# Up projection of a gated MLP: seven block products for eight over 6 of its 16 contraction tiles, with weight sums and two gating steps on POOL

## The chip, the cores and the metric

One core of a Trainium2 chip runs the whole layer in one launch. The metric is the device time of one execution in microseconds (us). The engines are PE (matmuls; PEld is its weight load), DVE, ACT, POOL and SP, which here only issues DMAs.

## What is computed

One layer of a diffusion block over 512 latent tokens, width 2048, in fp32. The part that matters here is the gated MLP at the end:

```
z = h @ w_up
grid = z.reshape(bsz, rows, GRID_W, 2 * D_FF)
...
val, gate = jnp.split(grid.reshape(bsz, n, 2 * D_FF), 2, axis=-1)
return (val * jax.nn.silu(gate)) @ w_down
```

`h` is 512 x 2048, `D_FF` is 5632, and the line left out is a depthwise 3 x 3 convolution over the 8 x 64 grid of tokens. The block's output is normalized and scaled by a row that comes from a product of the conditioning vector with a part of `w_ada`.

## The kernel before, in words

Every fp32 product is made of three matmuls (`mm3`, L175 to L178): both operands are split into a high and a low part, and hi x hi, hi x lo and lo x hi are added up in one PSUM bank. The split of activations is kept; weights are split on the way. `Stream` holds a list of weight **pages** in the order of use. `load` issues the DMA of a page into one of two `raw` tiles, `make` writes its high part on ACT (`whi`, L77) and the rest on DVE (`wlo`, L78). There are two `whi` and two `wlo` tiles, so the split of a page can begin only when PE has finished the page two before it, and `get` emits it one page ahead. All DMAs of pages are issued by SP, in order.

The hidden width is cut into 44 **blocks** of 128 channels. A block i has a value half (j = 0) and a gate half (j = 1). `up(i)` computes both: 4 pages of 1024 columns, 16 contraction tiles x 3 matmuls of 512 columns for each half, then ACT copies the bank into a padded tile `zp` (L1345). `conv(i)` does the 9 taps of both halves on DVE (L1309, L1311: 18 instructions), the SiLU on ACT (L1316), the product of the halves on DVE (L1318) and the split of the result `g` on ACT and DVE (L1323, L1325). `down(gi, d)` multiplies a group of four blocks with a quarter of `w_down`: 2 pages, 48 matmuls, four banks, which `evict` adds to `facc` on DVE (L1359). `up` and `down` alternate from block 5 on (`sched`); blocks 2 to 4, 42 and 43 have no `down` beside them, and five `down`s follow block 43.

Side work on DVE and ACT is written as generators and handed to `Threads`. `tick(us)` after some matmuls lets them emit as much work as 0.65 of that time pays for; `finish` emits a thread to its end at once. So the order on each engine is fixed when the program is built. One such thread is `gemv5`: 64 dot products on DVE (L975) of loaded rows of `w_ada` (`gv` tiles of 256 KB) with a row `srow2`, then `rows_of`, which turns the result into the rows `frow` that the last evictions need: DVE makes diagonals `dg`, PE multiplies them with ones (`rowb`), ACT copies them out. It is added before block 2 with the lowest priority.

Blocks 0 and 1 are computed earlier, in halves of 256 tokens (`up_half`, tiles `uh`).

## Time and profile before

| | |
|---|---|
| runs before | 2173.89, 2174.99, 2179.12 us (median 2174.99) |
| the profiled execution | 2177.72 us, its span 2175.9 us |
| busy share of the span | PE 97%, PEld 76%, DVE 69%, ACT 32%, POOL 11% |
| mean granted clock of PE | 0.983 of full |
| DMA | 315 MB, mean 145 GB/s |

The span is the time from the first to the last instruction. A busy PE is not a PE at its peak, since matmuls are pipelined: the distance between the starts of two matmuls says more than the duration of one. The MLP begins near 720 us and holds two thirds of the span.

### The profile page before, as it was taken

The numbers are of one execution on the slowest core, as the hardware profiler recorded it, in microseconds if no ns is written. First come the engines' busy times: TensorE is split into PE (matmuls) and PEld (weight loads), VectorE is DVE, ScalarE is ACT, GpSimd is POOL, SyncE is SP. The second block draws the span as 40 slices with busy tenths as digits, with TensorE's granted clock in tenths as the row PEclk, the third lists the DMA queues.
The fourth block names the chain that finished last, engine by engine and source line by source line (L and its number), as shares of the span: only waits on it lengthen the run. The fifth ranks groups of instructions, "written<-read, shape, count | busy, mean of one in ns | idle before, by whom it ended". The sixth has DMA issues, their size and how long they took to land.

```text
span 2175.9 us, 25243 instructions
## 1 busy us (share of the span) xinstructions
PE 2102.5 (97%) x9708; PEld 1645.7 (76%) x9708; DVE 1493.3 (69%) x2183; ACT 694.4 (32%) x976; POOL 243.8 (11%) x311
## 2 busy tenths in 40 slices
PE   7998999999898999999999999999999999999996
PEld 3575777767777888888888888888888888888885
DVE  1573488436677788778778777676776767767676
ACT  3343424544356323322222222222222222222224
POOL 5951100142025000000000000000000000000004
PEclk8999999999999999999999999999999999999998
DMA  9876454657665223443343333232332233232225
GB/s 371 311 285 218 136 178 145 205 150 206 223 211 204 78 88 127 144 140 119 109 154 124 124 126 112 88 97 88 97 97 92 93 97 93 92 97 97 92 93 193
DMA packets 107672, 315.05 MB, mean 145 GB/s; under 512 B 15520, under 2 KB 21536, under 8 KB 103328
## 3 DMA queue, kind: packets, MB, share of 16 engines
q1 hardware_dynamic: 99776, 303.39, 42.0%
q10 hardware_dynamic: 7776, 10.06, 1.4%
q8 instruction: 76, 1.25, 0.2%
q14 instruction: 44, 0.36, 0.0%
HBM read 302.46 MB, written 10.94 MB: 144 GB/s over the span
## 4 chain that ended last, share of the span: by engine, by line
PE 65%; DVE 2%; ACT 1%; issue 1%; DMA 1%; DVEq 0%; POOL 0%; ACTq 0%
PE up L176 14%; PE up L178 14%; PE up L177 14%; PE dn L177 7%; PE dn L178 7%; PE dn L176 7%; ACT scr L1124 1%; DMA raw<-in_w_up 0%; PE uh L178 0%; DMA raw<-in_w_down 0%; DVE facc L1126 0%; PE uh L177 0%; PE uh L176 0%; DVE wlo L78 0%; DVE hf L1195 0%
## 5 line engine op out<-in xcount | busy, mean ns | idle before, releaser
L78 DVE TENSOR_TENSOR wlo<-raw,whi 128x1024 fp32r<-128x1024 f32 (+1 forms) x326 | 403.6, 1239 | 456.7 <-ACT whi L77 453.9
L77 ACT ACTIVATE whi<-raw 128x1024 fp32r<-128x1024 f32 (+1 forms) x326 | 341.5, 1048 | 787.2 <-PE dn L178 308.6
L1311 DVE SCALAR_TENSOR_TENSOR cv<-zp,wconv,cv 128x512 f32<-128x512 f32 x704 | 528.4, 751 | 18.8
L176 PE MATMUL up<-h,whi 128*128 128x512 f32 x1344 | 531.4, 395 | 0.0
L178 PE MATMUL up<-h,wlo 128*128 128x512 f32 x1344 | 530.9, 395 | 0.0
L177 PE MATMUL up<-h,whi 128*128 128x512 f32 x1344 | 530.8, 395 | 0.0
L178 PEld LDWEIGHTS up<-h,wlo 128*128 128x128 f32 x1344 | 251.9, 187 | 61.8
L176 PEld LDWEIGHTS up<-h,whi 128*128 128x128 f32 x1344 | 252.0, 187 | 61.4
L177 PEld LDWEIGHTS up<-h,whi 128*128 128x128 f32 x1344 | 251.9, 187 | 61.4
L177 PE MATMUL dn<-wlo,g 128*128 128x512 f32 x672 | 265.5, 395 | 0.0
L178 PE MATMUL dn<-whi,g 128*128 128x512 f32 x672 | 265.4, 395 | 0.0
L176 PE MATMUL dn<-whi,g 128*128 128x512 f32 x672 | 265.4, 395 | 0.0
L1126 POOL TENSOR_TENSOR facc<-facc,frow 128x512 f32<-128x512 f32 x11 | 15.4, 1422 | 1435.1 <-ACT scr L1124 1435.1
L1345 ACT ACTIVATE zp<-up 128x512 f32<-128x512 f32 x84 | 50.5, 601 | 378.5 <-PE up L178 378.5
L177 PEld LDWEIGHTS dn<-wlo,g 128*128 128x128 f32 x672 | 126.0, 187 | 30.8
L176 PEld LDWEIGHTS dn<-whi,g 128*128 128x128 f32 x672 | 125.9, 187 | 30.9
L178 PEld LDWEIGHTS dn<-whi,g 128*128 128x128 f32 x672 | 126.0, 187 | 30.7
L975 DVE SCALAR_TENSOR_TENSOR scr<-gv,srow 128x512 bf16<-128x512 f32 x132 | 97.4, 738 | 17.8 <-DMA gv<-in_ada_n 11.1
L1359 DVE TENSOR_TENSOR facc<-facc,dn 128x512 f32<-128x512 f32 x144 | 92.1, 680 | 0.7 <-PE dn L178 0.7
L176 PE MATMUL ub<-hT,whi 128*128 128x512 f32 x192 | 79.4, 414 | 1.9 <-ACT mt L585 1.9
L176 PE MATMUL wo<-whi,mx 128*128 128x512 f32 x192 | 79.5, 414 | 0.0
L177 PE MATMUL wo<-wlo,mx 128*128 128x512 f32 x192 | 77.4, 403 | 0.9 <-DVE wlo L78 0.9
(285 smaller groups left out, 2434.4 us busy)
## 6 DMA issues: line engine op xcount, KB each, us to landing
raw<-in_w_up SPq DMA_DIRECT2D x176, 512.0 KB
raw<-in_w_down SPq DMA_DIRECT2D x88, 512.0 KB
gv<-in_ada_n SPq DMA_DIRECT2D x132, 256.0 KB
adak<-in_ada_k SPq DMA_DIRECT2D x32, 1024.0 KB
gv<-in_ada_m SPq DMA_DIRECT2D x96, 256.0 KB
raw<-in_w_out SPq DMA_DIRECT2D x32, 512.0 KB
raw<-in_w_inp SPq DMA_DIRECT2D x24, 512.0 KB
adag<-in_ada_n SPq DMA_DIRECT2D x7, 1024.0 KB
```

The costliest lines, as they stand in the source:

```text
L77: nc.scalar.activation(hi[:, :n], raw[:, :n], AF.Copy)
L78: nc.vector.tensor_tensor(lo[:, :n], raw[:, :n], hi[:, :n].bitcast(F32), op=OP.subtract)
L176: PE.matmul(o, ahi, bhi, start=start, stop=False)
L177: PE.matmul(o, ahi, blo, start=False, stop=False)
L178: PE.matmul(o, alo, bhi, start=False, stop=stop)
L975: V.scalar_tensor_tensor(scr[:, :512], tiles[x][:], 1.0, row(qf), op0=OP.mult, op1=OP.mult, accum_out=gacc[:, qf, c, nt:nt + 1])
L1124: S.activation(scr[:, :512], m, AF.Square, accum_out=st8[:, t, d:d + 1])
L1126: eng.tensor_tensor(m, m, row[d // 2][:, d % 2, :], op=OP.mult)
L1311: V.scalar_tensor_tensor(a[:], zz, wcol, a[:], op0=OP.mult, op1=OP.add)
L1345: S.activation(zp[j][i % 2][:, 1:9, 1:65], o.rearrange("p (r c) -> p r c", r=8), AF.Copy)
L1359: V.tensor_tensor(f, f, os[t], op=OP.add)
```

## The change

From block 4 on (`NS`), `up7(i)` takes the place of `up(i)`. Of the 16 contraction tiles, six (three of each half, `SW` = 3, brought to the front by `ORD`) are multiplied as 2 x 2 block matrices in Winograd's form of Strassen's scheme: rows are the value and gate half, columns are tokens 0 to 255 (`H0`) and 256 to 511 (`H1`), and the two contraction halves are the three tiles of each. Seven products of 3 tiles x 3 matmuls with 256 columns replace eight. The other ten tiles stay plain, in four pages of 640 columns. Sums of the activations are made once on POOL (`hsums`, in two parts before block 4), sums of the weights for each block on POOL (`make`, four instructions behind page `sb`), and the sums of the products by `csums` on DVE, from four banks into `zp`. Two steps of `conv` go from DVE to POOL. The weights of the six tiles come as a pair of tiles of 768 columns, one pair at a time (`load_pair`). `gemv5` begins before block 4 and has two `gv` tiles where it had four; `rows_of` follows block 43.

```
+            if key[0] == "sb":
+                (a11, a12), (a21, a22) = [(t[:, :SW * 128], t[:, SW * 128:]) for t in self.pair[key[1]]]
+                nc.gpsimd.tensor_tensor(a22, a21, a22, op=OP.add)
+                nc.gpsimd.tensor_tensor(a21, a11, a21, op=OP.subtract)
+                nc.gpsimd.tensor_tensor(a11, a22, a11, op=OP.subtract)
+                nc.gpsimd.tensor_tensor(a12, a12, a11, op=OP.subtract)
+            nxt = self.pairs.get(key)
+            if nxt is not None:
+                self.load_pair(*nxt)
...
+            pages += [(("up", i, 0), up[0]), (("sa", i), None), (("up", i, 2), up[2]), (("sb", i), None)]
+            pages += [(("up", i, 1), up[1]), (("up", i, 3), up[3]), (("sA", i), None), (("sB", i), None)]
...
+    W.pairs = {("sB", i): (i + 1, [A["w_ups"][i + 1 - NS, m] for m in range(2)]) for i in range(NS, NP - 1)}
...
     def conv(i):
         for j in range(2):
+            while i > 1 - j and not cth[i - 2 + j][2]:
+                bg._step(cth[i - 2 + j])
...
-        V.tensor_tensor(res[0][:], res[0][:], res[1][:], op=OP.mult)
+        PO.tensor_tensor(res[0][:], res[0][:], res[1][:], op=OP.mult)
...
-        V.tensor_tensor(g[:, 1, :], f, g[:, 0, :].bitcast(F32), op=OP.subtract)
+        PO.tensor_tensor(g[:, 1, :], f, g[:, 0, :].bitcast(F32), op=OP.subtract)
...
+    def csums(i, bk):
+        S.activation(z0[:, ha], v(p16[:, H0]), AF.Copy)
+        V.tensor_tensor(z1[:, ha], z0[:, ha], v(p16[:, H1]), op=OP.add)
+        V.tensor_tensor(z0[:, hb], z1[:, ha], v(p57[:, H0]), op=OP.add)
+        V.tensor_tensor(z1[:, ha], z1[:, ha], v(p57[:, H1]), op=OP.add)
+        V.tensor_tensor(z1[:, hb], z1[:, ha], v(p57[:, H0]), op=OP.add)
+        V.tensor_tensor(z0, z0, v(p23), op=OP.add)
+        V.tensor_tensor(z1, z1, v(yy), op=OP.add)
+        yield from conv(i)
...
+    def up7(i):
+        plain(p23, 0, 0)
+        w = W.get(("sa", i))
+        half(p16[:, H0], w, 0, lambda p: h2o[p][:, :, H0], True, False)
+        half(p23[:, H0], w, 1, lambda p: h2o[SW + p][:, :, H0], False, False)
+        plain(yy, 1, 0)
+        w = W.get(("sb", i))
+        half(yy[:, H0], w, 1, lambda p: tt["p", p][2], False, False)
+        plain(p23, 0, 1)
+        plain(yy, 1, 1)
+        w = W.get(("sA", i))
+        half(p16[:, H1], w, 0, lambda p: tt["p", p][1], False, True)
+        half(p23[:, H1], w, 1, lambda p: h2o[SW + p][:, :, H1], False, True)
+        w = W.get(("sB", i))
+        half(p57[:, H0], w, 1, lambda p: h2o[p][:, :, H1], True, False)
+        half(p57[:, H1], w, 0, lambda p: tt["p", p][0], False, True)
+        cth[i] = bg.add(csums(i, bk), 1)
+        if i == NP - 1:
+            fr2.append(bg.add(frows(), 0))
+    def frows():
+        bg.finish(g5_t)
+        while NP - 1 not in summed:
+            bg._step(cth[NP - 1])
+        yield from rows_of(3, frow, p2, "srow2", 1)
...
+            if x[1] == NH:
+                hs_t = bg.add(hsums(False), 0)
...
+            if x[1] == NS:
+                bg.finish(bg.add(hsums(True), 0))
+                g5_t = bg.add(gemv5(), 3)
```

`half` runs 3 tiles x 3 matmuls of 256 columns, `plain` 5 tiles x 3 of 512. In the names below, `up0`, `up2`, `up1`, `up3` are the four plain pages in their new order, `sa`, `sb`, `sA`, `sB` the pages made of the pair, `dn0` and `dn1` the two pages of a `down`.

**The order inside a block, on DVE.** Before (in the names: `cv` is a convolution, `facc` the sum of the down projection):

```order
L78 TENSOR_TENSOR wlo<-raw,whi 128x1024
L1311 SCALAR_TENSOR_TENSOR cv_11018<-zp_5553,wconv,cv_11018 128x512 x5
L78 TENSOR_TENSOR wlo<-raw,whi 128x1024
L1311 SCALAR_TENSOR_TENSOR cv_11018<-zp_5553,wconv,cv_11018 128x512
L1309 TENSOR_SCALAR cv_11080<-zp_5555,wconv 128x512
L1311 SCALAR_TENSOR_TENSOR cv_11080<-zp_5555,wconv,cv_11080 128x512
L1359 TENSOR_TENSOR facc_6407<-facc_6407,dn_11022 128x512
L1359 TENSOR_TENSOR facc_6408<-facc_6408,dn_11023 128x512
L1359 TENSOR_TENSOR facc_6409<-facc_6409,dn_11024 128x512
L78 TENSOR_TENSOR wlo<-raw,whi 128x1024
L1359 TENSOR_TENSOR facc_6410<-facc_6410,dn_11025 128x512
```

In the changed kernel, the same engine from page `sa` to page `sA` (`rs` are the tiles of the pair):

```order
L98 TENSOR_TENSOR wlo<-rs_12143,whi 128x768
L1401 SCALAR_TENSOR_TENSOR cv_12255<-zp_5553,wconv,cv_12255 128x512 x3
L98 TENSOR_TENSOR wlo<-raw,whi 128x640
L1401 SCALAR_TENSOR_TENSOR cv_12255<-zp_5553,wconv,cv_12255 128x512 x2
L98 TENSOR_TENSOR wlo<-rs_12144,whi 128x384
L1399 TENSOR_SCALAR cv_12351<-zp_5555,wconv 128x512
L1401 SCALAR_TENSOR_TENSOR cv_12351<-zp_5555,wconv,cv_12351 128x512 x2
L98 TENSOR_TENSOR wlo<-raw,whi 128x640
L1401 SCALAR_TENSOR_TENSOR cv_12351<-zp_5555,wconv,cv_12351 128x512
L98 TENSOR_TENSOR wlo<-raw,whi 128x640
L1401 SCALAR_TENSOR_TENSOR cv_12351<-zp_5555,wconv,cv_12351 128x512 x3
L98 TENSOR_TENSOR wlo<-rs_12143,whi 128x768
```

POOL, which had nothing between 4 memsets at the start of the MLP and the last evictions, in the changed kernel over the same block:

```order
L1408 TENSOR_TENSOR cv_12533<-cv_12533,cv_12629 128x512
L1415 TENSOR_TENSOR g<-cv_12533,g 128x512
L103 TENSOR_TENSOR rs_12700<-rs_12700 128x384
L104 TENSOR_TENSOR rs_12700<-rs_12699,rs_12700 128x384
L105 TENSOR_TENSOR rs_12699<-rs_12700,rs_12699 128x384
L106 TENSOR_TENSOR rs_12699<-rs_12699 128x384
```

Eight splits stand where four stood in a block's `up`, and the weight sums lie on POOL between the splits of `sb` and `sA`.

**The order of the loads, on SP.** Before, where the dot products still run:

```order
L172 DMA gv<-in_ada_n 128x512 x2
L60 DMA raw<-in_w_down 128x1024
L172 DMA gv<-in_ada_n 128x512
L60 DMA raw<-in_w_up 128x1024 x4
L172 DMA gv<-in_ada_n 128x512
L60 DMA raw<-in_w_down 128x1024 x2
```

In the changed kernel, one block:

```order
L68 DMA raw<-in_w_up 128x640
L204 DMA gv<-in_ada_n 128x512
L68 DMA raw<-in_w_up 128x640 x3
L68 DMA raw<-in_w_down 128x1024
L74 DMA rs_15760<-in_w_ups 128x768
L74 DMA rs_15761<-in_w_ups 128x768
L68 DMA raw<-in_w_down 128x1024
```

The pair of the next block is loaded between the two pages of the `down`.

**The end of `gemv5`, on DVE.** Before, its last dot product is row 956 of 1481, in the middle of the MLP, and behind block 43 stand only convolution, `facc` and splits:

```order
L1311 SCALAR_TENSOR_TENSOR cv_14854<-zp_5553,wconv,cv_14854 128x512 x3
L1359 TENSOR_TENSOR facc_6407<-facc_6407,dn_14857 128x512
L1359 TENSOR_TENSOR facc_6408<-facc_6408,dn_14858 128x512
L1359 TENSOR_TENSOR facc_6409<-facc_6409,dn_14859 128x512
L78 TENSOR_TENSOR wlo<-raw,whi 128x1024
L1359 TENSOR_TENSOR facc_6410<-facc_6410,dn_14860 128x512
L1309 TENSOR_SCALAR cv_14956<-zp_5555,wconv 128x512
```

In the changed kernel there is one dot product in each block, and behind block 43, after the split of `dn1`:

```order
L98 TENSOR_TENSOR wlo<-raw,whi 128x1024
L1015 SCALAR_TENSOR_TENSOR scr,gacc<-gv,srow_14436 128x512 x7
L1015 SCALAR_TENSOR_TENSOR scr,gacc<-gv,srow_17167 128x512 x16
L1059 TENSOR_TENSOR gacc<-gacc 128x2x16
L1060 TENSOR_TENSOR acol<-gacc 128x16
L1061 TENSOR_TENSOR acol<-acol,colp 128x16
L1063 TENSOR_TENSOR acol<-acol,colp 128x16
L1437 TENSOR_TENSOR zp_5555<-zp_5553,u_16926 128x4x64
L1438 TENSOR_TENSOR zp_5553<-zp_5555,u_16928 128x4x64
L1440 TENSOR_TENSOR zp_5555<-zp_5555,u_16928 128x4x64
L1441 TENSOR_TENSOR zp_5555<-zp_5555,u_16928 128x4x64
L1443 TENSOR_TENSOR zp_5553<-zp_5553,u_16927 128x8x64
```

23 of the 64 dot products now stand together; the diagonals `dg` follow two rows further down. On PE, the first `rowb` that reads them stands behind page `dn0` of the first `down` after block 43:

```order
L208 MATMUL dn_17129<-whi,g 128x512
L209 MATMUL dn_17129<-wlo,g 128x512
L210 MATMUL dn_17129<-whi,g 128x512
L1128 MATMUL rowb<-dg,ones 128x128 x4
L208 MATMUL dn_17126<-whi,g 128x512
```

Before, all `rowb` matmuls stood in the middle of the MLP.

## Rows read from the trace of the kernel before

**Rows 1.** Page, part 1: busy time, share of the span, instructions.
```profile
PE 2102.5 (97%) x9708; PEld 1645.7 (76%) x9708; DVE 1493.3 (69%) x2183; ACT 694.4 (32%) x976; POOL 243.8 (11%) x311
```
**Rows 2.** One stretch of the MLP: us; busy PE, PEld, DVE, ACT, POOL; clock; DMA share; GB/s.
```profile
1600.00:1800.00 200.00, 200.00 (x858) 160.65 (x857) 139.67 (x180) 49.49 (x60) 0.00 (x0) 1.00 0.30 95
```
**Rows 3.** Timeline of PE, end of blocks 0 and 1 (256 columns), start of block 2.
```profile
701.54 0.28 PE L176 MATMUL uh<-h,whi 128*128 128x256 f32 x1
...
720.79 0.39 PE L176 MATMUL up<-h,whi 128*128 128x512 f32 x1
...
727.32 0.40 PE L177 MATMUL up<-h,whi 128*128 128x512 f32 x1
```
**Rows 4.** Groups of DVE by form: count | busy us, mean ns | idle before, releasers.
```profile
L1311 DVE SCALAR_TENSOR_TENSOR cv<-zp,wconv,cv 128x512 f32<-128x512 f32 x704 | 528.4, 751 | 18.8
L975 DVE SCALAR_TENSOR_TENSOR scr<-gv,srow 128x512 bf16<-128x512 f32 x132 | 97.4, 738 | 17.8 <-DMA gv<-in_ada_n 11.1 <-ACT srow L1289 4.1 <-ACT scr L1124 0.9
L1359 DVE TENSOR_TENSOR facc<-facc,dn 128x512 f32<-128x512 f32 x144 | 92.1, 680 | 0.7 <-PE dn L178 0.7
L1195 DVE TENSOR_SCALAR hf<-h2p,acol 128x256 f32<-128x256 f32 x16 | 8.6, 538 | 1.3 <-POOL h L1197 1.3
L78 DVE TENSOR_TENSOR wlo<-raw,whi 128x768 fp32r<-128x768 f32 x4 | 3.8, 955 | 1.2 <-ACT whi L77 1.2
L78 DVE TENSOR_TENSOR wlo<-raw,whi 128x384 fp32r<-128x384 f32 x4 | 2.2, 552 | 0.5 <-ACT whi L77 0.5
```
**Rows 5.** Timeline of DVE inside one block of the MLP: start us, us, instruction, [idle before].
```profile
1700.03 1.23 DVE L78 TENSOR_TENSOR wlo<-raw,whi 128x1024 fp32r<-128x1024 f32 x1 [0.73 <-ACT whi L77]
1701.17 0.68 DVE L1359 TENSOR_TENSOR facc<-facc,dn 128x512 f32<-128x512 f32 x1
1701.77 3.10 DVE L1311 SCALAR_TENSOR_TENSOR cv<-zp,wconv,cv 128x512 f32<-128x512 f32 x4
...
1729.18 0.75 DVE L1311 SCALAR_TENSOR_TENSOR cv<-zp,wconv,cv 128x512 f32<-128x512 f32 x1
1729.84 0.48 DVE L1309 TENSOR_SCALAR cv<-zp,wconv 128x512 f32<-128x512 f32 x1
```
**Rows 6.** Timeline of DVE in the first stage, with POOL at work.
```profile
118.27 1.60 DVE L476 SCALAR_TENSOR_TENSOR xl<-xl,scsh,rst 128x512 f32<-128x512 f32 x1
119.79 1.60 DVE L484 SCALAR_TENSOR_TENSOR hT<-xl,scsh,hT 128x512 fp32r<-128x512 f32 x1
121.31 1.76 DVE L476 SCALAR_TENSOR_TENSOR xl<-xl,scsh,rst 128x512 f32<-128x512 f32 x1
```
**Rows 7.** Timeline of POOL: the same stretch, and the start of the last evictions.
```profile
117.75 1.56 POOL L564 TENSOR_TENSOR mi<-bb,pio 128x512 f32<-128x512 f32 x1
119.28 1.56 POOL L564 TENSOR_TENSOR tb<-bb,pio 128x512 f32<-128x512 f32 x1
...
2122.74 3.81 POOL L1126 TENSOR_TENSOR facc<-facc,frow 128x512 f32<-128x512 f32 x3 [1421.79 <-ACT scr L1124]
```
**Rows 8.** Timeline of POOL in the stage before the MLP.
```profile
661.24 6.89 POOL L1197 TENSOR_TENSOR h<-hf,h 128x256 fp32r<-128x256 f32 x9
```
**Rows 9.** Timeline of DVE in the last evictions: PSUM operand beside POOL, then SBUF.
```profile
2123.14 0.69 DVE L1123 TENSOR_TENSOR facc<-facc,dn 128x512 f32<-128x512 f32 x1 [0.64 <-PE dn L178]
2125.63 2.00 DVE L78 TENSOR_TENSOR wlo<-raw,whi 128x1024 fp32r<-128x1024 f32 x1 [1.80 <-ACT whi L77]
```
**Rows 10.** Timeline of SP: one page load of 512 KB is issued.
```profile
1717.90 0.33 SPq L60 DMA_DIRECT2D raw<-in_w_up  x1
```
**Rows 11.** Stretches of 1 us around that load; columns as in rows 2.
```profile
1718.00:1719.00 1.00, 1.00 (x6) 0.81 (x5) 0.96 (x3) 0.00 (x0) 0.00 (x0) 1.00 0.11 37
...
1720.00:1721.00 1.00, 1.00 (x6) 0.82 (x5) 0.45 (x1) 0.00 (x0) 0.00 (x0) 1.00 0.65 266
1721.00:1722.00 1.00, 1.00 (x6) 0.82 (x5) 0.00 (x0) 0.66 (x2) 0.00 (x0) 1.00 0.00 0
```
**Rows 12.** Groups of ACT, 1400 to 2000 us; columns as in rows 4.
```profile
L77 ACT ACTIVATE whi<-raw 128x1024 fp32r<-128x1024 f32 x107 | 113.2, 1058 | 287.8 <-PE dn L178 150.1 <-PE up L177 77.5 <-issue 60.2
```

More of the change, by code (lines that the diff above doesn't have):

```diff
@@ L41 @@
 NGRP = NP // GRP
+SW = 3
+PW = (16 - 2 * SW) * 64
+NS = 4
+ORD = [*range(SW), *range(8, 8 + SW), *range(SW, 8), *range(8 + SW, 16)]
 class Stream:
@@ L50, in __init__ @@
         self.raws, self.made, self.i = [], [], 0
+        self.pair, self.pairs = {}, {}
     def load(self, upto):
@@ L61, in load, with load_pair @@
             self.raws.append(raw)
+    def load_pair(self, i, aps):
+        self.pair[i] = [self.pool2.tile([128, SW * 256], F32, name=f"rs{m}", tag=f"rs{m}", bufs=1) for m in range(2)]
+        for t, ap in zip(self.pair[i], aps):
+            self.nc.sync.dma_start(t[:], ap)
     def make(self, upto):
@@ L68, in make @@
             self.load(i + 1 + self.dahead)
-            n = ap.shape[-1]
             raw = self.raws[i]
             self.raws[i] = None
+            c0 = 0
+            if key[0][0] == "s":
+                raw, n = self.pair[key[1]][key[0] in ("sb", "sB")], SW * 256
+                c0 = SW * 128 if key[0] == "sb" else 0
+                if key[0] == "sB":
+                    del self.pair[key[1]]
+            else:
+                n = ap.shape[-1]
             if key[0] in ("df", "wo2"):
@@ L970, in gv_dots @@
         for x in range(len(todo)):
-            while len(tiles) < min(x + 4, len(todo)):
+            while len(tiles) < min(x + gvp[1], len(todo)):
                 c, nt, qf = todo[len(tiles)]
@@ L1077, in rows_of @@
     def rows_of(c, r, pool, tag, bufs):
-        dgs = pool.tile([128, 1024], F32, name="dg", tag=tag, bufs=bufs)
+        nd = 8 if c == 0 else 4
+        dgs = pool.tile([128, nd * 128], F32, name="dg", tag=tag, bufs=bufs)
         for q in range(4):
@@ L1281, in emit @@
     gt = [None] * NP
-    frow = [pg(f"frow{j}", (2, 512)) for j in range(2)]
+    gvp[:] = [p2, 2]
+    W.pool2 = p2
+    frow = []
     def gemv5():
-        for hf in range(2):
-            sr = p2.tile([128, 1024], F32, name="srow2", tag="srow2", bufs=1)
-            nc.sync.dma_start(sr[:], A["c_row"][:, hf * 1024:(hf + 1) * 1024])
+        for qf in range(4):
+            sr = p2.tile([128, 512], F32, name="srow2", tag="srow2", bufs=1)
+            nc.sync.dma_start(sr[:], A["c_row"][:, qf * 512:(qf + 1) * 512])
@@ L1367, in down @@
         if gi == NGRP - 1:
-            bg.finish(g5_t)
+            bg.finish(*fr2)
+        bg.finish(*(ev_t if fr2 else ev_t[:-1]))
         os = [bank(f"dn{t}") for t in range(4)]
```

139 lines of the change are left out of this document (121 added, 18 removed).

## The prediction

> **What bounds the kernel now.** Read the page's first part before anything else: PE is busy 97% of the span, DVE 69%, POOL 11% [rows 1]. Then look at one stretch of the MLP alone: for 200 us PE never stops, at full granted clock, while DVE works 139.67 us and POOL nothing [rows 2]. So the MLP is bound by PE, and 60 us in 200 of DVE are free. Now take PE's pace from the distance between starts, not from durations. From 701.54 to 720.79 there are 165 matmuls of 256 columns, 0.1167 us each; from 720.79 to 727.32 there are 28 of 512 columns, 0.2333 us each [rows 3]. A matmul costs its columns and nothing else, so halving the columns loses nothing on PE.
>
> **PE's own saving.** A block loses 6 tiles x 2 halves x 3 = 36 matmuls of 512 columns, 8.40 us, and gets 7 x 3 x 3 = 63 of 256 columns, 7.35 us. That is 1.05 us for each of 40 blocks, 42 us if PE stays the bound. The Trainium skill (TensorE: Matmul & The Clock Gate, Back-to-back issue gap) gives N / 2.4 + 2.5 ns for a warm matmul of N columns; by that the block would save 0.89 us and the change 36 us. The rows decide for 1.05. A block with its down projection took 144 x 0.2333 = 33.6 us and would take 32.55.
>
> **What DVE gets.** Work that follows other work starts after 1.14 us for a split of 1024 columns, 0.60 for a `facc` addition, 0.78 for a convolution step behind its own kind (3.10 us for four), 0.66 before something else [rows 5]. From the splits of 768 and 384 columns [rows 4], a page of 640 takes 0.82 us, and about 0.08 less as a pitch. A block now has splits of 4 x 0.74, 3 x 0.87 and 0.47, 6.0 us for 4.6; sums of products 3.1 us (four of 256 columns at about 0.45, between the 0.68 and the 0.54 of the nearest PSUM readers [rows 4] less what the half length saves, two at 0.65); two gating steps less, 1.3 us. So DVE goes from about 24 to 27 us in a block of 32.55: by the sum alone it still fits.
>
> **What POOL does to DVE.** This is the dearest row. With POOL running, DVE's 512-column step with two SBUF inputs starts every 1.52 us instead of 0.66 (118.27, 119.79, 121.31), and POOL's own instructions start every 1.53 us [rows 6, 7]: they take turns. Undisturbed, POOL needs 3.81 / 3 = 1.27 us for 512 columns [rows 7] and 6.89 / 9 = 0.77 for 256 [rows 8], so about 1.0 for 384. A turn of POOL costs DVE 0.86 us at 512 columns; for 384 I take 0.75. An addition from PSUM is not touched: 0.69 us beside POOL, while a split of 1024 then takes 2.00 instead of 1.23 [rows 9, 5].
>
> **Where it hurts: page `up1`.** Its split on ACT can begin only when `up2` is done, and PE then has only `sb`, 9 x 0.1167 = 1.05 us, before it wants `up1` (two matmuls more, 0.47, before it wants the low part). ACT takes 0.7 of that (1.058 for 1024 [rows 12]), DVE 0.74: nothing is left over even without POOL. But just there POOL's four weight sums start, behind the split of `sb`. DVE has a first tap, two convolution steps and then the split of `up1`; three turns of POOL put 2.25 us between them.
>
> **The loop as a chain.** Follow it once around, from the end of PE's `up3`. ACT and DVE split `sB`: 1.8 us. Only then SP may issue the second tile of the next pair, whose buffer `sB` just left, and behind it the page `dn1`. A load of 512 KB issued at 1717.90 starts about 1 us later and has landed by 1721.1 [rows 10, 11]; 896 KB take between 3.7 and 4.8 us, say 4.3. Split of `dn1` on ACT and DVE: 2.3. Then DVE in order: a dot product and a turn of POOL (the product of the halves) 1.4, five sums 2.4, `up0` 0.74, the last sum 0.66, a first tap 0.5, three steps 2.2, `sa` 0.87, three steps 2.2, `up2` 0.74, two steps 1.45, `sb` 0.5: 13.7. The contended piece up to the split of `up1`: 0.5 + 2.25 + 1.45 + 0.74 = 4.9. PE's rest of `up1` and `up3`: 28 x 0.2333 = 6.5. Sum 33.5, with the hops between engines 33.7 us. So the chain, not PE's 32.55, sets the pace, and it equals the 33.6 of before: the 42 us are spent. Over the 37 blocks with a `down`: **+4 us**. Bounds: with POOL's first turn hidden beside the tap and the fast load, 32.9 (-26 us); with turns of a whole instruction and the slow load, 34.9 (+48).
>
> **Blocks without a `down`: 4, 42, 43.** DVE has there 13.4 of convolution, 6.0 of splits, 3.1 of sums and some 3.5 of POOL's turns, 26.0 us, PE 60 x 0.2333 + 63 x 0.1167 = 21.35; before, PE took 22.4 with DVE below it. +3.6 each. Block 4 also waits for POOL, which has 15 instructions of 256 columns to do behind block 3 before it may come to the weight sums, 12 to 16 us; +7. The 42 earlier ones run beside blocks 2 and 3 and are hidden there. Sum **+14** (0 to 25).
>
> **The end.** The dot products have the lowest priority and get one turn a block, so 23 are left when `frows` forces them out at once, behind the split of `dn1`. There were four `gv` tiles and are two now: a load waits for the dot product two before it, then takes about 1 + 1.1 us for 256 KB [rows 10, 11]. Two dot products in about 3.0 us. The first 2 are loaded, 5 take 7.6, the next row `srow2` waits for the last of them, is loaded and goes through a SiLU, 3, then 16 in 22: 35 us with the ends. Four small sums, six sums of block 43 and the diagonals: 4.6. The burst starts 2.3 us into the `down`. PE finishes `dn0` at 5.6 us and then stands before `rowb`, which reads the diagonals: **+36 us** of idle PE. Bounds: 19 if DVE alone paces it (23 x 0.61 and the rest), 47 if a load of 256 KB takes as long as one of 512.
>
> Sum +4 + 14 + 36 = +54 on the profiled execution's 2177.7 us, which lies 2.7 above the median: **2229, I say 2230 us.**
>
> **Rivals.**
> - *Faster.* POOL finds DVE's free time (60 us in 200 [rows 2]) and `up1` comes in time, so that the loop runs at 32.55; and the burst runs at DVE's pace. 2177.7 - 42 + 19 - 2.7 = 2152 us. For it: PE had no wait at all in that stretch. It decides by whether the low part of `up1` is ready 1.5 us after `up2` ends. Against it: three turns of POOL lie in front of it by the order. Chance 0.12.
> - *The same.* The loop gains its 42, the end costs its 36: 2177.7 - 42 + 36 - 2.7 = 2169, a little more with the blocks without a `down`. It needs only the first half of the rival above. 0.09.
> - *Slower still.* POOL's instruction keeps DVE out for its whole length. Then `up1` waits 3 x 1.0 and the product of the halves costs 1.3: the chain is 35.0 us, 37 x 1.4 = 52 more than before, with 14 and 36 about 2277 in all. The Trainium skill says just this (SBUF — State Buffer, Who interferes with whom): a DVE instruction with two SBUF inputs and a GpSimd instruction that reads SBUF exclude each other for a whole instruction, and the second blocks fully. The trace agrees on who is hit and on the taking of turns, but a turn costs 0.86 us where the instruction takes 1.27, so that part of it lies outside the lock. 0.18.
>
> **The numbers.** Forecast 0.61, by itself 2185 to 2270. The range of 2165 to 2290 takes in "the same" and the slow rival, and leaves out the fast one and the far ends. A difference under 0.3% cannot be told from none here (6.5 us). Faster 0.13, same 0.09, slower 0.78.
>
> **What would show it.** Right: PE waits for `wlo` once a block, for 0.5 to 1.5 us, at page `up1`; blocks 33 to 35 us apart; convolution steps above 1.4 us beside the weight sums; one idle time of PE of 20 to 45 us before `rowb`, some 100 us before the end. Wrong: PE without idle time in the loop (then the first two rivals), PE waiting for `dn1` or for `sA`, or no long wait at `rowb`.

## The result, and the profile after

The changed kernel takes 2290.4 us (median of 4 runs, 2286.8 to 2299.7) against 2174.4 for the kernel before (4 runs): a ratio of 1.054, 95% interval 1.050 to 1.057. It is slower, as forecast, but by 116 us where the forecast was 55 above the time before, and the time lies 0.4 us past the upper end of the range. The profiled execution took 2290.39 us, with a span of 2288.5, which is 112.6 more than the 2175.9 before.

First the page's part 1 of the changed kernel, to set beside [rows 1]:

```profile
PE 2098.1 (92%) x10788; PEld 1676.6 (73%) x10788; DVE 1777.3 (78%) x2495; ACT 737.4 (32%) x1098; POOL 651.1 (28%) x616
```

PE does about the same busy time and has 5% less of the span. DVE has not been relieved: 284 us more than before, and POOL 407 more. Now three stretches, with the columns of [rows 2] (us; busy PE, PEld, DVE, ACT, POOL; clock; DMA share; GB/s): blocks 4 and 5, the loop, and the end.

```profile
764.00:836.00 72.00, 53.35 (x254) 44.12 (x253) 62.95 (x73) 16.13 (x24) 34.42 (x29) 0.86 0.21 64
...
1600.00:1800.00 200.00, 191.06 (x976) 158.06 (x975) 178.93 (x235) 53.42 (x73) 49.07 (x36) 0.99 0.30 94
2100.00:2200.00 100.00, 53.32 (x270) 44.17 (x269) 67.99 (x124) 16.63 (x24) 16.17 (x12) 0.76 0.34 110
```

In [rows 2] PE was busy 200.00 of 200 us. It now stands still for 9 in 200 in the loop, for 19 of 72 in blocks 4 and 5, and for nearly half of the end, where the clock falls as well. The waits (engine and line waited for: us in total, times, longest) say for what:

```profile
ACT whi L97 <- DMA raw<-in_w_down: 125.8, 37, 5.5
...
PE u L210 <- DVE wlo L98: 60.8, 49, 2.8
...
PE rowb L1128 <- DVE dg L1124: 44.1, 2, 43.0
```

To see where 112.6 us went, take the start of PE's first matmul of each stage from both timelines (differences are taken before rounding):

| stage | before | after | difference | predicted |
|---|---|---|---|---|
| start to block 2 | 720.8 | 716.6 | -4.2 | 0 |
| blocks 2, 3 | 44.8 | 48.2 | +3.4 | 0 |
| blocks 4, 5 (no `down` between) | 44.8 | 70.6 | +25.8 | +7 |
| loop: 37 `down` and the 36 blocks between | 1224.3 | 1257.7 | +33.4 | +4 |
| blocks 42, 43 | 44.8 | 49.0 | +4.2 | +7 |
| `down` after block 43, up to `df` | 56.0 | 105.3 | +49.3 | +36 |
| `df` to the end | 40.4 | 41.0 | +0.7 | 0 |

The start is the same program up to small buffers, and block 2 began between 711 and 721 us in the kernels below, so the -4.2 is no finding. The rest is one place in every block, one pair of blocks, and one burst at the end.

**The place in every block.** The timeline of DVE around the split of `up1` in one block of the changed kernel (start us, us, instruction), then POOL's, then PE's waits, with those of a common block (1476.00) first:

```profile
1505.52 1.53 DVE L1401 SCALAR_TENSOR_TENSOR cv<-zp,wconv,cv 128x512 f32<-128x512 f32 x2
1506.97 0.55 DVE L98 TENSOR_TENSOR wlo<-rs,whi 128x384 fp32r<-128x384 f32 x1
1507.43 0.48 DVE L1399 TENSOR_SCALAR cv<-zp,wconv 128x512 f32<-128x512 f32 x1
1507.95 2.81 DVE L1401 SCALAR_TENSOR_TENSOR cv<-zp,wconv,cv 128x512 f32<-128x512 f32 x2
1510.68 1.61 DVE L98 TENSOR_TENSOR wlo<-raw,whi 128x640 fp32r<-128x640 f32 x1
...
1513.63 0.81 DVE L98 TENSOR_TENSOR wlo<-raw,whi 128x640 fp32r<-128x640 f32 x1
```

```profile
1507.60 1.19 POOL L103 TENSOR_TENSOR rs<-rs 128x384 f32<-128x384 f32 x1 [10.75 <-DVE wlo L98]
1508.86 1.35 POOL L104 TENSOR_TENSOR rs<-rs,rs 128x384 f32<-128x384 f32 x1
1510.29 1.32 POOL L105 TENSOR_TENSOR rs<-rs,rs 128x384 f32<-128x384 f32 x1
1511.69 1.47 POOL L106 TENSOR_TENSOR rs<-rs 128x384 f32<-128x384 f32 x1
```

```profile
1476.00 0.50 PE L210 MATMUL u<-h,wlo 128*128 128x512 f32 x1 [1.09 <-DVE wlo L98]
...
1512.35 0.50 PE L210 MATMUL u<-h,wlo 128*128 128x512 f32 x1 [1.87 <-DVE wlo L98]
```

Two convolution steps take 1.53 us ahead of the sums and 2.81 beside them; the split of 640 columns that PE waits for takes 1.61 us beside them, and that of the next page 0.81 just after. PE stands for 1.09 us in a common block, which is then 34.1 us long with its `down` (33.6 before). In the block shown the wait is 1.87 us, and the clock falls behind it. The next two stretches, with the columns us; busy PE; clock; DMA share; GB/s:

```profile
1512.00:1515.00 3.00, 2.65 (x8) 0.74 0.48 175
1515.00:1518.00 3.00, 3.00 (x11) 0.69 0.03 5
```

A mean of 0.74 over 3 us is 1.6 us at the lower level, 1.2 GHz, and 0.69 is 1.9. Five blocks of the loop, about 105 us apart, have their seven products in 24.0 to 25.6 us, where most have them in 22.7. PE waits there for 1.75 to 1.88 us. In four of them the clock then falls; in the one with 24.0 us it stays at full speed behind a wait as long as the one shown:

```profile
1723.35 0.50 PE L210 MATMUL u<-h,wlo 128*128 128x512 f32 x1 [1.87 <-DVE wlo L98]
...
1723.00:1726.00 3.00, 2.65 (x11) 1.00 0.49 168
```

So of the 2.9 us that the block shown is longer than a common one, some 1.6 us are the clock's, by the difference between the two blocks.

### The profile page after: what moved, and what is told of

Its sections match the earlier page's. It is cut to its first block, busy times and chain, and to the rows that moved or that the text cites. A ratio compares the mean times of both kernels' runs of the same rounds, so it can differ in the third digit from the quotient of the medians.

```text
span 2288.5 us, 28684 instructions
## 1 busy us (share of the span) xinstructions
PE 2098.1 (92%) x10788; PEld 1676.6 (73%) x10788; DVE 1777.3 (78%) x2495; ACT 737.4 (32%) x1098; POOL 651.1 (28%) x616
## 4 chain that ended last, share of the span: by engine, by line
PE 36%; DVE 21%; DMA 6%; issue 5%; ACT 3%; POOL 1%; SPq 0%; ACTq 0%; DVEq 0%; POOLq 0%
DVE wlo L98 8%; PE u L210 8%; PE u L208 8%; PE u L209 8%; DVE cv L1401 6%; DMA raw<-in_w_down 4%; PE dn L209 4%; PE dn L208 3%; PE dn L210 3%; ACT whi L97 2%; DVE scr L1015 2%; DMA gv<-in_ada_n 1%; DVE cv L1399 1%; DVE zp L1443 1%; DVE zp L1445 1%
## 5 line engine op out<-in xcount | busy, mean ns | idle before, releaser
L98 DVE TENSOR_TENSOR wlo<-raw,whi 128x1024 fp32r<-128x1024 f32 (+2 forms) x326 | 379.9, 1166 | 260.6 <-ACT whi L97 254.0
L210 PE MATMUL u<-h,wlo 128*128 128x512 f32 (+1 forms) x1280 | 460.4, 360 | 59.3 <-DVE wlo L98 58.9
L97 ACT ACTIVATE whi<-raw 128x1024 fp32r<-128x1024 f32 (+2 forms) x326 | 291.0, 893 | 661.0 <-PE u L209 265.3
L208 PE MATMUL u<-h,whi 128*128 128x512 f32 (+1 forms) x1280 | 455.4, 356 | 0.0
L209 PE MATMUL u<-h,whi 128*128 128x512 f32 (+1 forms) x1280 | 454.4, 355 | 0.0
L210 PEld LDWEIGHTS u<-h,wlo 128*128 128x128 f32 x1280 | 243.6, 190 | 115.9 <-DVE wlo L98 80.4
L97 ACT ACTIVATE whi<-rs 128x768 fp32r<-128x768 f32 (+1 forms) x160 | 122.8, 769 | 494.9 <-PE u L209 320.1
L209 PEld LDWEIGHTS u<-h,whi 128*128 128x128 f32 x1280 | 244.1, 191 | 35.5
L208 PEld LDWEIGHTS u<-h,whi 128*128 128x128 f32 x1280 | 244.1, 191 | 33.1
L98 DVE TENSOR_TENSOR wlo<-rs,whi 128x768 fp32r<-128x768 f32 (+1 forms) x160 | 138.0, 862 | 19.0 <-ACT whi L97 18.8
L208 PE MATMUL u<-ts,whi 128*128 128x256 f32 x360 | 101.7, 283 | 9.2 <-ACT whi L97 9.2
L210 PE MATMUL u<-ts,wlo 128*128 128x256 f32 x360 | 101.7, 283 | 1.9 <-DVE wlo L98 1.9
```

The costliest lines, as they stand in the source:

```text
L97: nc.scalar.activation(hi[:, c0:n], raw[:, c0:n], AF.Copy)
L98: nc.vector.tensor_tensor(lo[:, c0:n], raw[:, c0:n], hi[:, c0:n].bitcast(F32), op=OP.subtract)
L208: PE.matmul(o, ahi, bhi, start=start, stop=False)
L209: PE.matmul(o, ahi, blo, start=False, stop=False)
L210: PE.matmul(o, alo, bhi, start=False, stop=stop)
```

## The experiments

Every time is a median, beside the kernel before on the same chip (2173.9 to 2176.8 us in the five series). "Changed" is the changed kernel, 2290.4 us.

**No sums on POOL** (e1_no_sums)

```diff
...
-                nc.gpsimd.tensor_tensor(a22, a21, a22, op=OP.add)
...
-                nc.gpsimd.tensor_tensor(a12, a12, a11, op=OP.subtract)
+                pass
```

> The four sums of weights per block on POOL are left out (the blocks then use the loaded tiles as they are, so the up projection's values differ). Turn-taking (POOL's sums hold up DVE's steps in front of the split of the page up1): PE's wait for wlo at that page goes (60.8 us of it in 49 waits in the changed kernel), and with it the stretches at half clock behind the longest ones, so 45 to 60 us off 2290: 2230 to 2245 us, blocks about 33 us apart. Rival, the order of the pages: the split of up1 may only start when PE has done up2, and the sb piece covers just 1.05 us, so the wait stays without POOL: over 2275 us. Rival, DVE is full anyway (179 of 200 us busy): blocks stay at 34 us, over 2275 us.

2223.1 us, 67 less than changed and a little more than expected. The loop takes 1203.7 us instead of 1257.7, blocks 33.0 us with `u` at 21.6, blocks 4 and 5 62.1. The stretch of 1600 to 1800 us:

```profile
1600.00:1800.00 200.00, 199.78 (x1033) 165.84 (x1032) 169.50 (x244) 58.02 (x80) 18.89 (x13) 1.00 0.33 105
```

PE is bound again in the loop. So the sums make PE's wait there, and the order of pages alone doesn't. Whether they do so by their turns at one place, or by filling DVE, this run can't tell.

**More cover for `up1`** (e2_sb_in_up2_page)

```diff
+            elif key[0] == "sb":
+                hi, lo = self.made[-1][1:]
...
-        half(yy[:, H0], w, 1, lambda p: tt["p", p][2], False, False)
+        half(yy[:, H0], w, 0, lambda p: tt["p", p][2], False, False, PW)
```

> The split of the sb piece is written into the unused columns of the up2 page's buffers, so that the split of up1 needs only the buffer of sa, which is free 4.5 us before PE comes to up1, not 1.05 us. POOL's sums stay as they are. Theory: what costs time is POOL's turns together with that short cover; the wait for wlo at up1 goes, 40 to 60 us off: 2230 to 2250 us, though POOL still slows the convolution's steps. Rival, turn-taking costs DVE work that PE waits for later anyway (DVE is the engine that sets the 34 us): the wait only moves to another page, over 2275 us.

2295.6 us: nothing gained, and the wait is still at `up1`. ACT, DVE and PE in one block:

```profile
1442.51 0.74 ACT L101 ACTIVATE whi<-raw 128x640 fp32r<-128x640 f32 x1 [1.06 <-PE u L213]
...
1443.30 0.55 DVE L102 TENSOR_TENSOR wlo<-rs,whi 128x384 fp32r<-128x384 f32 x1
...
1443.77 0.48 DVE L1403 TENSOR_SCALAR cv<-zp,wconv 128x512 f32<-128x512 f32 x1
...
1444.28 2.81 DVE L1405 SCALAR_TENSOR_TENSOR cv<-zp,wconv,cv 128x512 f32<-128x512 f32 x2
...
1447.02 1.62 DVE L102 TENSOR_TENSOR wlo<-raw,whi 128x640 fp32r<-128x640 f32 x1
...
1448.70 0.50 PE L214 MATMUL u<-h,wlo 128*128 128x512 f32 x1 [1.08 <-DVE wlo L102]
```

ACT has its half of `up1` at 1443.25, over 3 us before PE comes to the page. DVE gets there at 1447.02, since its list has a first tap and two convolution steps in front. It is the order of DVE's list, made dear by POOL, that PE waits for; the short cover of the `sb` piece, on which the prediction leaned, was not it. The next edit tests this.

**`up1` right behind `sb`** (e7_up1_right_behind_sb: the edit above, and the convolution's steps elsewhere)

```diff
-        bg.tick(1.5)
-        plain(yy, 1, 0)
+        bg.tick(2.3)
+        plain(yy, 1, 0, 0.0)
...
-        bg.tick(0.7)
+        bg.tick(2.0)
...
```

> As e2_sb_in_up2_page, and the convolution steps that stood between the split of the sb piece and that of up1 are moved to other places of the block, so that DVE makes the split of up1 at once. Theory: the wait is made of the convolution steps that DVE has in front of that split, each of them longer beside POOL's sums; with the order changed PE finds up1 ready, the waits and the stretches at half clock behind them go, 40 to 60 us less than 2290: 2230 to 2250 us. Rival: DVE has too much to do in these stretches wherever the split stands, and PE waits as long at the next page, up3: over 2275 us.

2256.5 us, 34 less than changed and 39 less than the edit above, a little short of what was expected. PE's wait for `wlo` falls from 60.8 to 23.2 us in all; some blocks reach `u` = 21.6 us and others 22.9, with waits at other pieces.

**The pair behind `dn1`** (e5_pair_behind_dn1)

```diff
-    W.pairs = {("sB", i): (i + 1, [A["w_ups"][i + 1 - NS, m] for m in range(2)]) for i in range(NS, NP - 1)}
+    W.pairs = {}
+    for x, y in zip(sched, sched[1:]):
+        if x[0] == "U" and NS <= x[1] < NP - 1:
+            i = x[1]
+            key = ("sB", i) if y[0] == "U" else ("dn", y[1], y[2], 0)
+            W.pairs[key] = (i + 1, [A["w_ups"][i + 1 - NS, m] for m in range(2)])
```

> The next block's pair of tiles is loaded behind both pages of the down projection instead of between them, which is where ACT's split of the second one waits (125.8 us in 37 waits in the changed kernel). Theory of the prediction: this delay of about 2 us a block runs on through DVE's list to the split of up1 and is part of the 0.5 to 1.1 us that each block is longer; without it 10 to 25 us less: 2265 to 2280 us. Rival, now the likelier, since blocks without the weight sums came out 33.0 us long with this wait unchanged (132.6 us): it costs PE nothing, 2285 to 2295 us.

2270.2 us, 20 less: the time is the theory's, though for most blocks the rival holds. In the changed kernel SP issues `dn1` behind the pair, and ACT takes it up so (a common block, then the one whose wait was 1.87):

```profile
1450.71 0.42 SPq L68 DMA_DIRECT2D raw<-in_w_down  x1
...
1484.84 0.42 SPq L68 DMA_DIRECT2D raw<-in_w_down  x1
```

```profile
1454.72 1.06 ACT L97 ACTIVATE whi<-raw 128x1024 fp32r<-128x1024 f32 x1 [2.97 <-DMA raw<-in_w_down]
...
1491.34 1.06 ACT L97 ACTIVATE whi<-raw 128x1024 fp32r<-128x1024 f32 x1 [5.47 <-DMA raw<-in_w_down]
```

From issue to use this takes 4.0 us, and 6.5 in the block that loses its clock. Over the loop it is 3.9 to 4.9 us, and 5.1 to 6.5 in front of the five long blocks. With the pair loaded later those blocks, with `u` of 24 to 25.6 us, are gone. But the common block stays at 34.1: PE's wait at `up1` is 1.05 us in nearly every block, for 1.09. DVE's last idle time in front of the split of `up1`, and that split, in the changed kernel and then with the pair loaded later:

```profile
1455.81 1.23 DVE L98 TENSOR_TENSOR wlo<-raw,whi 128x1024 fp32r<-128x1024 f32 x1 [2.21 <-ACT whi L97]
...
1474.32 1.63 DVE L98 TENSOR_TENSOR wlo<-raw,whi 128x640 fp32r<-128x640 f32 x1
```

```profile
1459.30 0.85 ACT L97 ACTIVATE whi<-rs 128x768 fp32r<-128x768 f32 x1 [4.33 <-PE dn L210]
...
1460.18 0.96 DVE L98 TENSOR_TENSOR wlo<-rs,whi 128x768 fp32r<-128x768 f32 x1 [1.08 <-ACT whi L97]
...
1469.25 1.64 DVE L98 TENSOR_TENSOR wlo<-raw,whi 128x640 fp32r<-128x640 f32 x1
```

In the changed kernel DVE waits for `dn1`, behind the load, and works without a pause from there to `up1`. With the load earlier it waits at `sa` instead, for ACT, and ACT for PE's end of the `down`; from there to `up1` its list is the same. So two paths of nearly equal length lead to the wait, and taking one away gains 0.04 us in a common block. The load behind the pair cost time in five blocks, by a longer wait and by the clock behind it.

**Dot products: by priority (e3_dots_spread), then at fixed places (e8_dots_fixed_places)**

```diff
-                yield 0.8, 0.5
+                yield 0.8, 2.5
...
-                g5_t = bg.add(gemv5(), 3)
+                g5_t = bg.add(gemv5(), 0.5)
```

> The 64 dot products of the last modulation row come two to a block from block 4 on instead of at the very end of DVE's list, so that none are left before the rows of the last gate. Theory: the burst of 23 of them is PE's one idle time of 43 us; it goes, and the end is 40 to 50 us shorter, against up to 10 us that the loop gets longer: 2240 to 2258 us. Rival: the last block's convolution, not the dot products, is what the rows wait for, and 20 us or more of the wait stay: over 2265 us.

2461.4 us, 171 more: the theory falls, and not for the rival's reason. The end did what was expected (5.6 us from the `down` to `rowb` instead of 49.0), but in the loop each `down` took 17 us instead of 11.4. ACT, DVE and PE in one of them:

```profile
1599.10 1.06 ACT L97 ACTIVATE whi<-raw 128x1024 fp32r<-128x1024 f32 x1 [5.27 <-DMA raw<-in_w_down]
1600.19 1.23 DVE L98 TENSOR_TENSOR wlo<-raw,whi 128x1024 fp32r<-128x1024 f32 x1 [4.43 <-ACT whi L97]
...
1602.00 1.87 DVE L1536 TENSOR_TENSOR facc<-facc,dn 128x512 f32<-128x512 f32 x3
1602.73 0.80 PE L208 MATMUL dn<-whi,g 128*128 128x512 f32 x1 [6.14 <-DVE facc L1536]
```

The dot products used up the share of a tick, the evictions of the last `down` slid behind the split of `dn1`, that split waits for its load, and PE needs the banks.

At fixed places (the second number of `yield`, the pages that `tick` lets pass before the thread's next step, keeps the shares from emitting them):

```diff
-                yield 0.8, 0.5
+                yield 0.8, 1000.0
...
+        if not g5_t[2]:
+            bg._step(g5_t)
         w = W.get(("sA", i))
...
+        if not g5_t[2]:
+            bg._step(g5_t)
         w = W.get(("sB", i))
```

> The 64 dot products are issued two to a block from block 4 on, at two fixed places (in front of the splits of sA's and sB's successors), apart from the shares that set the order of everything else, so that the evictions of the down projection keep their places, which they lost when the dot products came by priority. Theory: the end is 43 us shorter, and the loop pays at most 23 more dot products of 0.7 us on an engine with slack: 2245 to 2265 us. Rival: any dot product in front of a split costs PE its duration, 64 times 0.7 us is 45 us: 2275 to 2300 us.

2250.4 us, 40 less, as the theory had it: 5.8 us from the `down` to `rowb`, where it was 49.0, and a loop only some 6 us longer. The burst is the end's cost.

**The late sums behind the first weight sums** (e4_late_sums_behind)

```diff
-                bg.finish(bg.add(hsums(True), 0))
...
         half(yy[:, H0], w, 1, lambda p: tt["p", p][2], False, False)
+        if i == NS:
+            bg.finish(bg.add(hsums(True), 0))
```

> The late sums of columns (15 instructions, 16.4 us on POOL) are issued behind the first four sums of weights, inside block 4, instead of ahead of it. Theory: blocks 4 and 5 are 25.8 us longer than before because the weight sums stand behind them in POOL's queue; PE needs the late sums only for the last piece of the block, some 10 us later, so that 8 to 15 us of it go: 2275 to 2282 us. Rival: the long wait is for the product and gating steps of the convolution on POOL, which come out the same: 2287 us or more. Rival: the late sums are then what PE waits for at the last piece, as long as before: 2287 us or more, with the wait at the sB piece in place of that at sA.

2291.8 us; blocks 4 and 5 take 70.5 us for 70.6. The theory falls, and the second rival holds: in block 4 PE stands for POOL's late sums in either order. In the changed kernel the weight sums, and with them the split of `sA`, stand behind them; in this one PE waits for a late sum itself, at `sB`:

```profile
790.44 1.58 ACT L97 ACTIVATE whi<-rs 128x768 fp32r<-128x768 f32 x2 [12.37 <-POOL rs L106]
...
791.33 0.58 PE L208 MATMUL u<-ts,whi 128*128 128x256 f32 x1 [3.87 <-ACT whi L97]
```

```profile
796.77 0.58 PE L208 MATMUL u<-h,whi 128*128 128x256 f32 x1 [3.07 <-POOL h L1364]
```

Block 4 takes 33.5 us and block 5 37.0. In block 5 the long wait is another one (changed kernel):

```profile
816.81 6.26 DVE L1401 SCALAR_TENSOR_TENSOR cv<-zp,wconv,cv 128x512 f32<-128x512 f32 x8
...
823.10 0.63 ACT L1406 ACTIVATE cv<-cv 128x512 f32<-128x512 f32 x1 [11.62 <-DVE cv L1401]
...
826.53 0.58 PE L208 MATMUL u<-ts,whi 128*128 128x256 f32 x1 [5.36 <-ACT whi L97]
```

DVE does eight convolution steps in a row, which `conv` forces because the second accumulator `cv1` has one buffer; the SiLU on ACT waits for them, and the split of `sA` stands behind it.

**Two buffers for the second accumulator** (e9_cv1_two)

```diff
-    gvp[:] = [p2, 2]
+    gvp[:] = [p2, 1]
...
-            while i > 1 - j and not cth[i - 2 + j][2]:
-                bg._step(cth[i - 2 + j])
+            while i > 1 and not cth[i - 2][2]:
+                bg._step(cth[i - 2])
...
-            a = p2.tile([128, 8, 64], F32, name=f"cv{j}", tag=f"cv{j}", bufs=2 - j)
+            a = p2.tile([128, 8, 64], F32, name=f"cv{j}", tag=f"cv{j}", bufs=2)
```

> The second accumulator of the convolution has two buffers again, as before the change (the tile of the dot products gets one buffer instead of two to make room), so that a convolution need not be finished before the next one's second half may start. Theory: in blocks 4 and 5 DVE does eight forced steps in a row, ACT's split of sA stands behind the silu of that convolution, and PE waits 5.4 us; with two buffers the steps can stay behind and that wait goes: the two blocks 8 to 15 us shorter, 2275 to 2283 us. Rival: DVE is full there (105 of 115 us), and the steps are only late at another place, 2287 us or more; the dot products may also wait for their loads, and then it is over 2295 us.

2330.1 us. Blocks 4 and 5 shrink to 58.3, block 5 alone from 37.0 to 25.5, so that the forced steps were its wait. But the `down` behind them grows from 11.2 to 21.9: the steps are only late at another place. The rest is the dot products, each of which now waits for its own load:

```profile
PE rowb L1128 <- DVE dg L1124: 80.0, 2, 79.4
```

**Plain blocks up to block 5** (e10_plain_to_block_5)

```diff
-NS = 4
+NS = 6
```

> The seven products begin with block 6, so that blocks 4 and 5, which have no down projection between them, are computed plainly as before (64 products of whole width instead of the seven; two blocks fewer gain the 1.05 us). Theory: without a down projection PE's block is 22.4 us or less, DVE's work for the seven products with POOL's turns is more than that, and so DVE is the bound in blocks 4 and 5 alone (105 of 115 us busy); with plain blocks there the 70.6 us shrink to 45 to 52: 2266 to 2273 us. Rival: the backlog only moves on to blocks 6 and 7, which lose what was won: 2280 us or more. Rival: the late sums on POOL are the cause, and come just as hard in front of block 6: 2280 us or more, with the wait at block 6.

2271.1 us, 19 less, the time that was expected, but only about half of it by these blocks. Blocks 2 to 5 take 93.0 us together, 25.8 less; blocks 6 and 7 inherit 16 of them, 32.6 and 28.9 us with their seven products for 22.7 later on, so that the rival is right in part. The profiled execution has the rest of its lead from a start that was 6 us shorter and from fewer long blocks later in the loop (two of 24 us or more for five), which this edit does not touch.

**The gating steps, three ways** (first e6_gating_dve)

```diff
-        PO.tensor_tensor(res[0][:], res[0][:], res[1][:], op=OP.mult)
+        V.tensor_tensor(res[0][:], res[0][:], res[1][:], op=OP.mult)
...
-        PO.tensor_tensor(g[:, 1, :], f, g[:, 0, :].bitcast(F32), op=OP.subtract)
+        V.tensor_tensor(g[:, 1, :], f, g[:, 0, :].bitcast(F32), op=OP.subtract)
```

> The two gating steps are back on DVE, as before the change; the sums of weights stay on POOL. Theory: they cost DVE 1.4 us a block there and 1.7 us of turns beside POOL (two turns of 0.86 us) where they stand now, so that moving them made no difference to PE in the loop: within 12 us of 2290, 2278 to 2302 us. Rival, they are a second cause beside the sums (they too slow the steps in front of a split): 2278 us or less. Rival, DVE is so full that 1.4 us more a block come through one for one: over 2310 us.

2475.4 us, 185 more: far over what even the rival gave. The same edit with the pair behind both pages:

> The gating steps on DVE as in e6_gating_dve (2475 us there), and the pair loaded behind both pages of the down projection. Theory: the 185 us of e6_gating_dve come from the order: one to two evictions of the down projection stand behind the split of its second page, which waits for a load behind the pair, and PE needs their PSUM; with the load earlier the down projections take 11.4 to 12.5 us instead of 17, 2270 to 2310 us. Rival, DVE is full with the gating steps: still over 2400 us.

2332.2 us. The wait for evictions in the two:

```profile
PE dn L208 <- DVE facc L1536: 119.8, 33, 5.6
```

```profile
PE dn L208 <- DVE facc L1541: 40.6, 33, 1.3
```

So most of the 185 us is the slide that the dot products showed, evictions behind a split that waits for a load. The kernel to set beside the second one is that with the pair behind `dn1` alone, 2270.2 us: with the load out of the way, the two gating steps on DVE still cost 62 us, 1.7 us a block, where they take 1.4 on DVE. So they come through in full, as the last rival expected for e6_gating_dve had it, and moving them to POOL was worth its turns here. And the other way round, the kernel before with the gating steps on POOL, alone:

> The kernel before with one part of the change alone: its two gating steps on POOL instead of DVE. Theory: DVE has 60 us of 200 to spare there and PE is bound, so that two turns a block hurt nobody: 2165 to 2182 us, no change. Rival: any work of POOL beside DVE's splits makes PE wait: over 2190 us.

2175.1 us, ratio 0.9999, interval 0.9987 to 1.0012. This part of the change by itself costs nothing where DVE has room.

**The sums on DVE** (e14_sums_on_dve)

```diff
-                nc.gpsimd.tensor_tensor(a22, a21, a22, op=OP.add)
+                nc.vector.tensor_tensor(a22, a21, a22, op=OP.add)
```

(and the other three)

> The changed kernel with its four sums of weights a block on DVE instead of POOL, at the same place in the program. POOL's turns cost DVE about 2.7 us a block (16 convolution steps by 0.13 us, six splits by 0.11 us, from the means with and without the sums); the sums themselves cost DVE some 1.9 us (four by half of the 0.95 us of a 768-column split). Theory: DVE gains 0.8 us a block and PE some of it: 2262 to 2285 us. Rival: what counts is the work in front of up1's split alone, 1.9 us of sums against up to three turns of 0.86 us: within 8 us of 2290 us. Rival: nothing of the turns was on PE's path and the sums come on top: over 2300 us.

2309.7 us, 19 more. The theory falls; the time is the last rival's, but not its reason, since the turns were on PE's path (no sums at all: 2223.1). In this place the four sums, 0.56 us each, are 2.2 us in front of the split of `up1`, against 2.1 in turns (1.28 for the two steps, 0.80 for the split). Common blocks have `u` of 23.0 us for 22.7, and more blocks are long: nine of 24 us or more for five.

**Together** (e12_together, then e13, e15 and e17)

The edits that gained, in one kernel: the pair behind `dn1`, `up1` behind `sb`, plain blocks to block 5, and dot products at fixed places (other ones than above).

> The edits that each took time away, together: the pair loaded behind both pages of the down projection, the split of up1 right behind that of sb (whose piece lies in the free columns of the up2 page), the dot products at two fixed places of the blocks, and plain blocks up to block 5. If the four causes are separate and the loop comes to 33.0 to 33.3 us a block, its 36 blocks are 10 to 20 us shorter than before the change, against some 10 us that blocks 2 and 3, 42 and 43 and the end stay longer: 2160 to 2180 us, about the time before. Rival: DVE, at 94 to 96% of the period of 33 us, is the next bound, blocks stay at 33.8 us or more: 2185 to 2210 us.

2221.9 us, above both. Blocks stay at 34.2 us, as the rival had it, but not because DVE is full: in one block (1443 to 1477 us) it had 2.9 us of idle time, waiting for ACT. The wait of PE had moved on to the pieces `sA` and `sB`, behind a dot product and three convolution steps. The next kernel moves those, and lets the plain blocks do more of the convolution (part of the edit):

```diff
+            if j == 1 and NS in cth:
+                dot()
             whi, wlo = W.get(("dn", gi, d, j))
...
-        bg.tick(2.2)
+        bg.tick(1.5)
         w = W.get(("sB", i))
...
```

> As e12_together, with the dot products at places where DVE waits for ACT's splits (in front of the first page of the next block, and at the start of the block), one convolution step moved from between sA's and sB's splits to behind them, and a larger share of convolution steps in the plain blocks 2 to 5, so that less of them is left for blocks 6 and 7. Theory, the order of DVE's list: PE's waits at sA and sB (0.5 to 1.1 us a block) go, blocks near 33.2 us, blocks 6 and 7 some 10 us shorter: 2180 to 2200 us. Rival, DVE is full beside POOL's turns: the wait appears at another page, blocks stay at 34 us: over 2210 us.

2183.7 us, as expected, and with the sums on DVE behind the split of `up1`:

> As e13_other_places, with the four sums of weights on DVE, right behind the split of up1. Theory: without turns DVE has about 0.8 us a block less to do, and PE comes near the 33.0 us that blocks had without any sums: 2170 to 2190 us. Rival: the 1.9 us of sums in a row in front of up3's split make PE wait there: over 2200 us.

2176.3 us, also as expected. The stretch of 1600 to 1800 us, sums on POOL and then on DVE, and the convolution's group from 1400 to 1800 in each:

```profile
1600.00:1800.00 200.00, 200.00 (x1038) 167.91 (x1037) 185.76 (x255) 57.31 (x80) 54.97 (x36) 1.00 0.35 112
...
L1410 DVE SCALAR_TENSOR_TENSOR cv<-zp,wconv,cv 128x512 f32<-128x512 f32 x195 | 172.0, 882 | 4.8
```

```profile
1600.00:1800.00 200.00, 200.00 (x1042) 168.25 (x1041) 182.78 (x280) 57.72 (x80) 20.83 (x12) 1.00 0.35 111
...
L1410 DVE SCALAR_TENSOR_TENSOR cv<-zp,wconv,cv 128x512 f32<-128x512 f32 x197 | 147.8, 750 | 4.8
```

PE has no idle time in either, with DVE at 93 and 91%. So DVE was not full at 34.1 us a block: the order was the bound. And DVE, which POOL was to relieve, is busier with the sums on POOL than with the sums on itself. What was left stood mostly in the first block of the loop: in the second kernel, in block 6, ACT and PE:

```profile
844.45 0.63 ACT L1340 ACTIVATE srow<-srow 128x512 f32<-128x512 f32 x1 [11.77 <-DMA srow<-in_c_row]
...
845.86 0.58 PE L211 MATMUL u<-h,whi 128*128 128x256 f32 x1 [9.30 <-ACT whi L101]
```

The first row for the dot products uses the late sums' tile, and the splits stand behind it on ACT. One more kernel starts them a block later:

> As e15_other_places_sums_on_dve, with the dot products beginning a block later and the convolution's old share in the plain blocks 2 to 5. Theory: PE's 9.3 us in block 6 are ACT's wait for the first row of the dot products, whose tile is the late sums' own, and go; the plain blocks come back from 100 to 93 us, against 2 to 3 us more in blocks 6 and 7: 2158 to 2168 us, 0.3 to 0.8% faster than before the change. Rival: the late sums on POOL or the backlog of the convolution hold block 6 as long without the row: 2170 us or more.

2164.7 us (9 runs), as expected: ratio 0.9955, interval 0.9938 to 0.9972, so 0.45% faster than the kernel before, a small gain but clear of the noise. PE's wait of 9.3 us is gone. The loop takes 1201.1 us for the 1224.3 before; 12 of these 23 us go back, 3.2 in blocks 2 to 5, 1.3 in blocks 42 and 43 and 7.9 in the end.

## Why the prediction was wrong in size, by its own steps

The sum was +54, and the spans differ by 112.6. Of what was missed, 29 us are in the loop, 19 in blocks 4 and 5 and 13 in the end; the other stages give 3 back.

- **PE's own saving, 1.05 us a block: right.** In the two kernels with the sums on DVE and no wait of PE in the loop, `u` is 21.35 us, for 22.40 before: 1.05. The rule of the Trainium skill weighed there (TensorE: Matmul & The Clock Gate, Back-to-back issue gap) gives a saving of 0.89 us; the runs decide against it. A `down` takes 11.4 instead of 11.2, so that a block comes to 32.8 us, not 32.55.
- **What POOL does to DVE: right in kind, a little dear.** A turn beside the 384-column sums cost (2.81 - 1.53) / 2 = 0.64 us; I took 0.75.
- **The loop as a chain, +4 us: this step failed in size.** It measured +33.4, inside its bounds. The chain itself is there: a common block is 34.1 us where I had 33.7. The 0.4 us are mostly turns of POOL's gating steps: the dot product beside the first of them takes 1.7 us (1456.95 to 1458.66) where I had 1.4, and the split of `up0` beside the second, which the sum did not price, 1.0 instead of 0.74 (1460.96 to 1461.96). Over 36 blocks that is about one half. The other half is five blocks 2 to 4 us longer than 33.6, for two things the sum left out: the load behind the pair, taken as 4.3 us throughout, takes 5.1 to 6.5 there, and behind four of the waits of 1.75 to 1.88 us PE goes on at 1.2 GHz for some 3 us. Moving that load took 20 us off. What the chain also did not see is a second path as long as itself, from the end of the `down` through `sa`, so that without the load a common block is no shorter. The split of `up1` was the right place, by the right mechanism; but the cover of 1.05 us, of which the text made much, did not matter. DVE was late by its order even with ACT's half done 3 us before PE came.
- **Blocks without a `down`, +14: failed.** Blocks 42 and 43 came to +4.2 for 7.2. Block 4 came to +11.1 for 7, and POOL's late sums are on its path, as I had it (16.5 us, 767.98 to 784.44, behind which PE stands 3.9 us); how long it would be without them no run shows. The step that failed is block 5, which the sum put at nothing without a reason and which measured +14.6: DVE comes there with convolutions still to do, is forced to eight steps in a row, and PE waits 5.4 us behind them. Plain blocks there gave some 10 us back, counted over blocks 4 to 7.
- **The 42 earlier sums hidden: nearly.** Blocks 2 and 3 are 3.4 us longer.
- **The end, +36: right in kind, too small.** PE waited 43.0 us in one piece before `rowb`, as described. The dot products were the mis-sized term: the last 16 took 27.0 us (2159.99 to 2186.96), where I had 22, and all 23 took 42.5 for 35. Two more things were left out. The first matmuls afterwards run at the lower clock: the 12 of the `down` behind the first eight `rowb` take 4.4 us for 2.8. And the 32 `rowb` themselves, some 3 us, stood in the loop before and stand in the end now.
- **The rivals.** "Slower still", at 2277, came nearest to the time, for another reason: DVE was not kept out for a whole instruction of POOL (1.19 to 1.47 us), but 0.64. The rule of the Trainium skill quoted there (SBUF — State Buffer, Who interferes with whom) says the whole instruction; these rows agree with it on who is hit, not on how long. "Faster" named the right test for the loop (the low part of `up1` in time), and the last kernel shows what it takes.
